# Matmuls on zeros, in thirteen orders of the moving operand, between the warm-up and the first product of a two-block kernel

## The chip, the cores and the metric

One core of a Trainium2 chip runs one program. The metric is the device time of one execution, in microseconds. Before the change it is 2994.82 us, the median of three runs (2993.81 to 2994.98).

## The reference, cut to what matters

256 tokens of 2048 features go through two transformer blocks, in float32:

```python
def forward(x, ...):
    for i in range(2):          # first block: an even layer, then an odd one
        h = rmsnorm(x, g)       # even: sparse top-k and dilated attention; odd: stick-breaking and forgetting
        x = x + (attention(h @ w_in) * silu(gate)) @ w_out
    x = rmsnorm(x, norm_f)
    # second block: swiglu feed-forward, NSA attention beside a gated recurrence, swiglu, per-layer embedding
    ...
```

Nearly all the arithmetic is in the products with the weight matrices. The change adds nothing to what is computed: none of its results is read.

## The kernel before, in words

**Products.** Every weight matrix is cut into panels of up to 512 columns, and a panel into tiles of two chunks of 128 rows (128x1024 values, 512 KB). `run_stream` walks over these tiles in order. The activations are kept transposed, split into a high part `hi` and a rest `lo` (`to_act`, lines 251 to 258: TensorE transposes into PSUM on line 247, ScalarE writes `hi`, VectorE writes `lo`). A weight tile is split in the same way by `cut` (lines 324 and 325: ScalarE writes `wh`, VectorE `wl`). For each chunk and each of the two halves of the tokens, `product` issues three matmuls (lines 366 to 368): hi times wh, hi times wl, lo times wh. So a chunk takes six matmuls, each with 512 float32r columns as the moving operand in contiguous order and its own weight load.

**Order.** The order of the instructions on each engine is the order of the Python code. Work beside the products waits in queues of closures (`soon`, `paced`, `back`) from which `run_stream` takes one at fixed points; after the first chunk of a tile it takes one from `paced`.

**The start.** SyncE's queue first gets the gains `nrow`, then in turn pieces of the input (`load_x`, eight of 256 KB) and the first five weight tiles (`load`, at most `RAWB` = 5 at a time). `start` fills a bfloat16 tile `wu` with zeros on VectorE, and `warm(WARM)` multiplies it with itself eight times (line 525). A transpose then brings the gains into a column layout (`g0T`). After that `run_stream` runs, for i = 0, 1, 2: the transposes and splits of input piece i (`first[i]`), `FILL[i]` = 4, 2, 0 more warm-up matmuls, the load of tile 5 + i and the split of tile i. Then the products begin; the transposes of pieces 3 to 7 come out of `paced`, one per tile.

**Buffers.** Tiles of 128x1024 float32 come out of a pool of 27 (`blk`); PSUM tiles for everything but the products come out of a pool of four (`aux`).

**One other line that the prediction uses.** Line 1345 (`cmp_blocks`) is a VectorE addition far behind the start; it reads every sixteenth value of one tile, and each value of the other operand 15 times. Lines 1223 and 488 are VectorE products over contiguous values.

Of the kernel before, what the change touches and what calls it, by code (L numbers as in the profile page):

```python
# [11 lines left out]
F32 = mybir.dt.float32  # L12
F32R = mybir.dt.float32r
# [6 lines left out]
P = 128  # L20
T = 256
D = 2048
# [13 lines left out]
# columns of the float32 constants  # L36
# [8 lines left out]
# columns of the bfloat16 constants  # L45
# [69 lines left out]
class Act:  # L115
    """Transposed activations, split: chunk c is a pair of [128, 256] float32r views."""
# [8 lines left out]
def two_blocks_kernel(ctx, tc, a, out):  # L125
# [43 lines left out]
    # residual stream, natural: h[p] is [128 tokens, 2, 512 columns]  # L169
# [8 lines left out]
    def load_x(i):  # L178
        """columns of two chunks of x"""
        v = slice(i % 2 * T, i % 2 * T + T)  # L180
        nc.sync.dma_start(h[i // 2][:, :, v], xs[:, :, i * T:i * T + T])
# [20 lines left out]
    def sums(parts, n, s):  # L202
        """room for partial sums of squares [128, 2, parts] and, behind them, n * eps"""
        t = cp.tile([P, 2, parts + 1], F32, name=s)
        nc.gpsimd.memset(t[:, :, parts:parts + 1], n * EPS)
        return t

    def rsq(ssq, s):
        """(sum of the parts of ssq) ** -0.5, as [128, 2]"""
        tot = small([P, 2], s)  # L210
        nc.vector.tensor_reduce(tot, ssq, axis=AX.X, op=ALU.add)
        r = cp.tile([P, 2], F32, name=nm(s))
        nc.gpsimd.tensor_tensor(r, tot, mhalf, op=ALU.pow)
        return r
# [22 lines left out]
    def to_act(src, act, c0, n, gain):  # L237
        """src: natural [128, 2, n * 128]; chunks c0.. of act (within a group of four), scaled per feature by
        gain(c)."""
        hi, lo = act_block(act, c0 // 4)  # L240
        b = c0 % 4
        for j in range(0, n, 2):
            w = min(2, n - j)
            tp = aux()
            for i in range(w):
                for t in range(2):
                    nc.tensor.transpose(tp[:, i * 256 + t * P:i * 256 + t * P + P],  # L247
                                        src[:, t, (j + i) * P:(j + i + 1) * P], ident)
            if gain is None:
                tv = tp[:, :w * 256].rearrange("p (c q) -> p c q", q=256)  # L250
                nc.scalar.activation(hi[:, b + j:b + j + w], tv, AF.Copy)  # L251
                nc.vector.tensor_tensor(lo[:, b + j:b + j + w], tv, hi[:, b + j:b + j + w], op=ALU.subtract)  # L252
            else:
                for i in range(w):
                    nc.scalar.activation(hi[:, b + j + i], tp[:, i * 256:i * 256 + 256], AF.Copy,  # L255
                                         scale=gain(c0 + j + i))
                for i in range(w):
                    nc.vector.scalar_tensor_tensor(lo[:, b + j + i], tp[:, i * 256:i * 256 + 256], gain(c0 + j + i),  # L258
                                                   hi[:, b + j + i], op0=ALU.mult, op1=ALU.subtract)
            for i in range(w):  # L260
                act.hi[c0 + j + i] = hi[:, b + j + i]
                act.lo[c0 + j + i] = lo[:, b + j + i]
# [10 lines left out]
    def panel(w, n0, n1, groups, act, done, coff=0, rate=1, pre=None, late=False, hold=0):  # L273
        # hold: chunks in whose shadow nothing of the paced queue is started
        """x-stationary product of act with w[:, n0:n1]; groups: lists of chunks, in order."""
        panels.append(dict(w=w.rearrange("(c p) n -> p c n", p=P), n0=n0, n1=n1, groups=groups, act=act,
                           done=done, coff=coff, rate=rate, pre=pre, late=late, hold=hold, raw=None))
# [8 lines left out]
    def run_stream():  # L286
# [56 lines left out]
        for s, (pl, cs, first, slot_end, last) in enumerate(tiles):  # L343
# [9 lines left out]
            else:  # L353
# [16 lines left out]
                if n <= P:  # L370
                    # narrow panel, held whole: one tile of tokens after the other
                    held.append((cs, wh, wl))
                    if last:
                        seq = [(c, wh, wl, j) for cs, wh, wl in held for j, c in enumerate(cs)]
                        held = []
                        for t in range(2):
                            for i, x in enumerate(seq):
                                product(t, *x, i == 0, i == len(seq) - 1)
                    cs_ = ()
                else:  # L380
                    cs_ = cs
# [25 lines left out]
    def pipeline(units, depth, between={}):  # L407
        """units: lists of `depth` closures; one closure per slot, each unit's steps in successive slots."""
        for i in range(len(units) + depth - 1):
            def go(i=i):  # L410
                for d in range(depth - 1, -1, -1):
                    if 0 <= i - d < len(units):
                        units[i - d][d]()
            back.append(go)
            if i in between:
                back.append(between[i])

# [1 line left out]
    def softmax_unit(qT, kT, v, bias, evac, mult=None, extra=None, full=False):  # L419
        """qT(), kT(): [128, 256]; v(kt): [128 keys, 128]; bias: [128, 384] bf16 (queries of tile 0 x keys of  # L420
        tile 0 | queries of tile 1 x all keys); evac(t, psum, 1 / sum)."""
# [53 lines left out]
    def rope_nat(src, dst, c0, nh, half, cn, sn, dup=False):  # L475
        """Rotate heads of 2 * half columns at src[:, t, c0:]; write to dst at the same columns."""
# [14 lines left out]
    def heads_T(src, cols, dst, scale=1.0):  # L491
        """Transpose the 128-column slices src[:, t, c] (c in cols) into dst(i): [128, 256]; pairs share a bank."""
# [14 lines left out]
    # =====================================================================  # L507
    # start: gains, input, statistics
    # =====================================================================
# [4 lines left out]

    def start():
        # the clocks of the tensor engine and the activation tables are up before the first data arrive
# [6 lines left out]
        def warm(n):  # L523
            for _ in range(n):
                mm(tpw, wu[:, 0:P], wu, start=True, stop=True)
        warm(WARM)
        tp0 = aux()
# [29 lines left out]
    # =====================================================================  # L557
    # layer_even
    # =====================================================================
# [174 lines left out]
    # residual update by a panel of a product, then the next layer's operand  # L734
# [22 lines left out]
    # =====================================================================  # L757
    # layer_odd
    # =====================================================================
# [94 lines left out]
    def odd_gate(j, c0, c1):  # L854
        """columns c0:c1 of the gate; panel 0 also carries the forget logits in front."""
# [61 lines left out]
    def load_gain(name):  # L917
        """a gain on all partitions, two blocks of 1024 columns"""
# [36 lines left out]
    # =====================================================================  # L955
    # feed-forward layers
    # =====================================================================
# [50 lines left out]
    def post_norm_panel(y, ssq, i, gname, f):  # L1008
        """sums of squares of a finished panel; the panel times the gain and f * sqrt(D)."""
# [12 lines left out]
    def post_norm(y, ssq, last_gain, act, gain, ss_next, rkey):  # L1022
        """h += normed y; next operand, two chunks at a time."""
# [56 lines left out]
    # =====================================================================  # L1080
    # mixer
    # =====================================================================
# [43 lines left out]
    def pre_mix4():  # L1126
        # 8 * softplus(-lambda), with log1p(e) = 2 atanh(e / (2 + e))
# [39 lines left out]
    def rope_part(n, c0, nh):  # L1167
        """rotate the first 32 columns of heads at n[:, t, c0:], in place"""
# [138 lines left out]
    KV = {"kc0": 0, "kc1": 1, "vc0": 2, "vc1": 3, "ks0": 4, "ks1": 5, "kw0": 6, "kw1": 7}  # L1307

    def mix_kv(items, post=None):
        """items: (column, kind, name); k kinds are rotated and transposed, vT transposed, v kept."""  # L1310
# [39 lines left out]
    def cmp_panel(wname, which):  # L1350
        st = {}

        def fn(i, rawt):
# [6 lines left out]
            if i == 7:  # L1360
                # gelu(2y) = (1 + tanh(2 sqrt(2 / pi) (1 + 4 * 0.044715 y^2) y)) y
# [9 lines left out]
                def fin1():  # L1371
# [6 lines left out]
                    def fin2():  # L1378
                        po = aux()
                        w2 = KM["w2"]  # L1380
                        if which == 0:
                            for c in range(2):
                                mm(po[:, 0:30], w2[:, 0, c], hT[:, c], start=c == 0, stop=c == 1)
                            # the keys of head h at columns 16 h .. 16 h + 14 of row block h
# [40 lines left out]
    def nsa_cmp():  # L1425
        """attention to the compressed keys, all heads, added to the other two"""
# [51 lines left out]
    def nsa_heads(j):  # L1478
        """attention of four heads to the selected blocks and to the window"""
# [84 lines left out]
    # =====================================================================  # L1564
    # second feed-forward, per-layer embedding
    # =====================================================================
# [72 lines left out]
```

## Time and profile before

| what | value |
|---|---|
| median of three runs | 2994.82 us (2993.81 to 2994.98) |
| span of the profiled execution, first to last instruction | 2991.7 us |
| time outside the span, by difference to the median | 3.1 us |
| TensorE busy (matmuls) | 2969.3 us, 99% |
| VectorE busy | 1611.1 us, 54% |
| ScalarE busy | 1439.6 us, 48% |
| mean DMA rate | 178 GB/s |

The profile gives no time of its own for the profiled execution beyond the span; the runs are not the profiled execution, and the 3.1 us is a difference between the two. Matmuls are pipelined: the duration of one in the rows reaches past the start of the next one, so the cost of a matmul in a stream is the step from one start to the next, not its duration. In a row that merges several, the time is that from the first start to the last end.

### The profile page before, as it was taken

The page shows a single profiled execution, that of the slowest core. Times are in us where ns is not written, and L with a number is a line of the kernel's source. Part 1 is how long each engine was busy: PE and PEld are TensorE (multiplying, and loading weights), DVE is VectorE, ACT ScalarE, POOL GpSimd, SP SyncE. Part 2 cuts the span into 40 slices and gives each one's busy share as a digit, 9 for nine tenths or more (in the row PEclk, how much of TensorE's full clock was granted, in tenths as well). Part 3 has the DMA queues.
Part 4 walks back from the last instruction along what each step waited for, and adds up shares of the span by engine and source line. Part 5 has one row for each costly group of instructions (what it writes and reads, how often), then busy time and mean ns, then how long its engine had stood idle before and what let it go on. Part 6 is the DMA issues. An engine that isn't in the chain of part 4 may idle for free. (4 is left out here: it accounts for less than half of the span.)

```text
span 2991.7 us, 36158 instructions
## 1 busy us (share of the span) xinstructions
PE 2969.3 (99%) x13805; PEld 2436.2 (81%) x13805; DVE 1611.1 (54%) x2126; ACT 1439.6 (48%) x1961; POOL 38.3 (1%) x83
## 2 busy tenths in 40 slices
PE   9999999999999999999999999999999999999998
PEld 7788888888998888888888887887888888888787
DVE  5675554444455554454454565666644445454565
ACT  5545545484554544443434464555544443443464
POOL 1000000000000000000000010000000000000000
PEclk9999999999999999999999999999999999999999
DMA  7555566646555666656666556644565665656654
GB/s 229 157 173 151 156 183 177 184 140 180 147 180 181 191 182 187 188 183 186 185 185 200 180 156 196 197 152 134 170 183 187 185 189 184 185 185 200 182 171 146
DMA packets 289038, 531.59 MB, mean 178 GB/s; under 512 B 17328, under 2 KB 60704, under 8 KB 288864
## 3 DMA queue, kind: packets, MB, share of 16 engines
q1 hardware_dynamic: 285184, 520.04, 57.8%
q0 software_dynamic: 2960, 8.13, 0.8%
q8 instruction: 108, 1.77, 0.2%
q10 hardware_dynamic: 720, 1.11, 0.1%
q14 instruction: 66, 0.54, 0.1%
HBM read 527.11 MB, written 2.10 MB: 177 GB/s over the span
## 5 line engine op out<-in xcount | busy, mean ns | idle before, releaser
L325 DVE TENSOR_TENSOR wl<-raw,wh 128x1024 fp32r<-128x1024 f32 (+5 forms) x994 | 1184.2, 1198 | 1052.4 <-ACT wh L324 1045.8
L324 ACT ACTIVATE wh<-raw 128x1024 fp32r<-128x1024 f32 (+5 forms) x994 | 1025.1, 1037 | 1097.3 <-PE mm L368 1054.0
L366 PE MATMUL mm<-wh,hi 128*128 128x512 f32 (+4 forms) x3968 | 1548.4, 390 | 1.1 <-ACT hi L255 0.6
L368 PE MATMUL mm<-wh,lo 128*128 128x512 f32 (+4 forms) x3968 | 1547.2, 390 | 1.0 <-DVE lo L258 1.0
L367 PE MATMUL mm<-wl,hi 128*128 128x512 f32 (+4 forms) x3968 | 1535.3, 387 | 1.4 <-DVE wl L325 1.1
L367 PEld LDWEIGHTS mm<-wl,hi 128*128 128x128 f32 x3968 | 746.3, 188 | 165.0 <-DVE wl L325 3.8
L366 PEld LDWEIGHTS mm<-wh,hi 128*128 128x128 f32 x3968 | 746.0, 188 | 157.1 <-issue 3.3
L368 PEld LDWEIGHTS mm<-wh,lo 128*128 128x128 f32 x3968 | 745.6, 188 | 156.5 <-DVE lo L258 2.9
L252 DVE TENSOR_TENSOR lo<-ax,hi 128x512 fp32r<-128x512 f32 x61 | 39.3, 686 | 47.1 <-ACT hi L251 47.1
L251 ACT ACTIVATE hi<-ax 128x512 fp32r<-128x512 f32 x61 | 33.2, 595 | 63.9 <-PE ax L247 63.9
L255 ACT ACTIVATE hi<-ax,gT 128x256 fp32r<-128x256 f32 x72 | 29.5, 472 | 40.4 <-PE ax L247 40.4
L446 ACT ACTIVATE e<-ax,m 128x128 f32<-128x128 f32 x68 | 28.0, 416 | 42.7 <-DVE m L443 42.6
L461 ACT ACTIVATE pT<-ax 128x384 f32<-128x384 f32 x40 | 19.5, 488 | 47.5 <-PE ax L459 47.2
L996 DVE TENSOR_TENSOR y<-mm,y 128x512 f32<-128x512 f32 (+2 forms) x52 | 32.0, 644 | 15.7 <-PE mm L368 15.6
L443 DVE TENSOR_REDUCE m<-ax 128x1 f32<-128x128 f32 x80 | 24.7, 351 | 25.2 <-PE ax L434 17.1
L258 DVE SCALAR_TENSOR_TENSOR lo<-ax,gT,hi 128x256 fp32r<-128x256 f32 x72 | 30.9, 477 | 12.9 <-ACT hi L255 12.8
L229 ACT ACTIVATE junk<-h 128x512 f32<-128x512 f32 x56 | 35.5, 634 | 2.5 <-DVE h L934 1.1
L247 PE MATMUL ax<-cf,h 128*128 128x128 f32 x192 | 29.1, 278 | 7.5 <-DMA h<-in_x_dram 3.6
L247 PEld LDWEIGHTS ax<-cf,h 128*128 128x128 f32 x192 | 23.2, 142 | 15.6 <-issue 6.1
L452 DVE RECIPROCAL rl<-l 128x2 f32<-128x2 f32 x40 | 6.6, 166 | 46.6 <-ACT e L446 46.4
L1359 PE MATMUL ax<-raw,cb 128*30 128x256 f32 x128 | 28.6, 380 | 0.0
L366 PE MATMUL mm<-wh,rhi 128*128 128x512 f32 x64 | 27.6, 431 | 0.0
(392 smaller groups left out, 1231.1 us busy)
## 6 DMA issues: line engine op xcount, KB each, us to landing
raw<-in_w_in_dram SPq DMA_DIRECT2D x239, 512.0 KB, 3.7
raw<-in_ff_w_gate_dram SPq DMA_DIRECT2D x176, 512.0 KB, 3.8
raw<-in_ff_w_up_dram SPq DMA_DIRECT2D x176, 512.0 KB, 3.8
raw<-in_ff_w_down_dram SPq DMA_DIRECT2D x170, 512.0 KB, 3.6
raw<-in_w_out_dram SPq DMA_DIRECT2D x93, 512.0 KB, 4.0
raw<-in_w_ple_gate_dram SPq DMA_DIRECT2D x26, 512.0 KB, 4.3
raw<-in_w_in_dram SPq DMA_DIRECT2D x32, 384.0 KB, 3.6
raw<-in_w_in_dram SPq DMA_DIRECT2D x24, 412.0 KB, 3.5
```

Of the source, the lines that this page charges most:

```text
L229: nc.scalar.activation(j[:, :src.shape[2]], src[:, t], AF.Square, accum_out=ssq[:, t, p:p + 1])
L247: nc.tensor.transpose(tp[:, i * 256 + t * P:i * 256 + t * P + P], src[:, t, (j + i) * P:(j + i + 1) * P], ident)
L251: nc.scalar.activation(hi[:, b + j:b + j + w], tv, AF.Copy)
L252: nc.vector.tensor_tensor(lo[:, b + j:b + j + w], tv, hi[:, b + j:b + j + w], op=ALU.subtract)
L255: nc.scalar.activation(hi[:, b + j + i], tp[:, i * 256:i * 256 + 256], AF.Copy, scale=gain(c0 + j + i))
L258: nc.vector.scalar_tensor_tensor(lo[:, b + j + i], tp[:, i * 256:i * 256 + 256], gain(c0 + j + i), hi[:, b + j + i], op0=ALU.mult, op1=ALU ...
L324: nc.scalar.activation(wh[:, k], v[:, k], AF.Copy)
L325: nc.vector.tensor_tensor(wl[:, k], v[:, k], wh[:, k], op=ALU.subtract)
L366: mm(o, xh[:, q], wh[:, j], start=first, stop=False)
L367: mm(o, xh[:, q], wl[:, j], start=False, stop=False)
L368: mm(o, xl[:, q], wh[:, j], start=False, stop=last)
L996: nc.vector.tensor_tensor(v[:, t], pt[t], v[:, t], op=ALU.add)
```

## The change

Between `warm(WARM)` and the transpose of the gains, `start` calls a new function. It takes two of the 27 blocks (`x` as stationary, `y` as moving operand, float32r), a bfloat16 tile of its own and one PSUM tile, fills the three SBUF tiles with zeros on VectorE, and runs the same list twice: thirteen groups of float32r matmuls, nine in the first group and six in each of the others, then six bfloat16 matmuls. By the code these are 2 x (9 + 12 x 6 + 6) = 174 matmuls. The rest of the diff takes out comments and docstrings.

```diff
+    def strides(out):
+        x, y = blk("px", F32R), blk("py", F32R)
+        xb = cp.tile([P, 512], BF16, name="pxb")
+        nc.vector.memset(x.bitcast(F32), 0.0)
+        nc.vector.memset(y.bitcast(F32), 0.0)
+        nc.vector.memset(xb, 0.0)
+        out2 = aux()
+
+        def run(m, cols=P, n=6, two=False, same=False):
+            size = 1
+            for k in m.shape[1:]:
+                size *= k
+            for i in range(n):
+                o = (out2 if two and i % 2 else out)[0:cols, 0:size]
+                j = 0 if same else i % 4
+                mm(o, x[:, j * P:j * P + cols], m, start=True, stop=True)
+
+        for _ in range(2):
+            run(y[:, 0:512], n=9)
+            run(y[:, 2:514])
+            run(y.rearrange("p (a b) -> p a b", b=32)[:, :, 0:16])
+            run(y.rearrange("p (a b) -> p a b", b=4)[:, :, 0:2])
+            run(y.rearrange("p (a b) -> p a b", b=8)[:, :, 0:4])
+            run(y[:, None, 0:16].to_broadcast([P, 32, 16]))
+            run(y.rearrange("p (s a b) -> p a s b", s=4, b=16)[:, 0:8])
+            run(y.rearrange("p (s a b) -> p a s b", s=2, b=16)[:, 0:16])
+            run(y.rearrange("p (s a b) -> p a s b", s=2, b=2)[:, 0:128])
+            run(y[:, 0:256])
+            run(y[:, 0:512], cols=96)
+            run(y[:, 0:512], two=True)
+            run(y[:, 0:512], same=True)
+            for _ in range(6):
+                mm(out, xb[:, 0:P], xb, start=True, stop=True)
+
     def start():
...
         warm(WARM)
+        strides(tpw)
         tp0 = aux()
         nc.tensor.transpose(tp0[:, 0:16], nrow, ident[0:16, 0:16])
```

Twelve of the thirteen groups have 512 columns, one has 256. Seven read `y` in pieces: runs of 16 values with gaps of 16, runs of 2 with gaps of 2, runs of 4 with gaps of 4, the same 16 values 32 times, runs of 16 from four quarters in turn, runs of 16 from two halves in turn, runs of 2 from two halves in turn.

## Rows read from the trace of the kernel before

**Rows 1.** The page's first part: span; engine, busy us, share, instructions.

```profile
span 2991.7 us, 36158 instructions
PE 2969.3 (99%) x13805; PEld 2436.2 (81%) x13805; DVE 1611.1 (54%) x2126; ACT 1439.6 (48%) x1961; POOL 38.3 (1%) x83
```

**Rows 2.** Busy time by stretch, all engines; the columns are named in the first line.

```profile
core 0: us, PE busy (x) PEld busy (x) DVE busy (x) ACT busy (x) POOL busy (x), PEclk, DMA share, GB/s
5.00:10.00 5.00, 3.15 (x16) 1.78 (x16) 3.19 (x8) 3.71 (x7) 3.04 (x7) 1.00 1.00 337
10.00:15.00 5.00, 2.00 (x10) 1.38 (x10) 3.18 (x4) 1.90 (x3) 2.92 (x19) 1.00 1.04 395
15.00:20.00 5.00, 4.63 (x16) 3.75 (x17) 2.21 (x4) 2.84 (x4) 0.00 (x0) 0.66 1.08 359
500.00:1000.00 500.00, 500.00 (x2423) 425.20 (x2422) 243.14 (x295) 274.66 (x386) 5.92 (x9) 1.00 0.57 170
```

**Rows 3.** Timeline of TensorE's start: start us, us, instruction, [idle before <-releaser].

```profile
1.19 3.60 PE L525 MATMUL ax<-wu 128*128 128x512 bf16 x8 [1.19 <-DVE wu L518]
4.93 1.12 PE L247 MATMUL ax<-cf,h 128*128 128x128 f32 x4
7.70 0.59 PE L525 MATMUL ax<-wu 128*128 128x512 bf16 x2
10.35 0.48 PE L366 MATMUL mm<-wh,hi 128*128 128x512 f32 x1
15.37 0.63 PE L247 MATMUL ax<-cf,h 128*128 128x128 f32 x4 [3.37 <-DMA h<-in_x_dram]
17.08 0.63 PE L367 MATMUL mm<-wl,hi 128*128 128x512 f32 x1
17.50 0.63 PE L368 MATMUL mm<-wh,lo 128*128 128x512 f32 x1
20.18 0.60 PE L247 MATMUL ax<-cf,h 128*128 128x128 f32 x4
20.53 0.48 PE L366 MATMUL mm<-wh,hi 128*128 128x512 f32 x1
```

**Rows 4.** The same view at 500 us: first and last of nine 512-column matmuls.

```profile
499.74 0.39 PE L366 MATMUL mm<-wh,hi 128*128 128x512 f32 x1
501.60 0.40 PE L368 MATMUL mm<-wh,lo 128*128 128x512 f32 x1
```

**Rows 5.** The same view at 1850 us: first and last of nine 384-column matmuls.

```profile
1849.97 0.34 PE L366 MATMUL mm<-wh,hi 128*128 128x384 f32 x1
1851.38 0.34 PE L368 MATMUL mm<-wh,lo 128*128 128x384 f32 x1
```

**Rows 6.** The same view for VectorE and ScalarE in the start.

```profile
0.86 0.27 DVE L518 MEMSET wu<- 128x256 uint32 x1 [0.86 <-PEq L1627]
6.09 0.84 ACT L255 ACTIVATE hi<-ax,g0T 128x256 fp32r<-128x256 f32 x2 [3.41 <-PE ax L247]
7.75 1.28 DVE L325 TENSOR_TENSOR wl<-raw,wh 128x512 fp32r<-128x512 f32 x2
9.85 1.23 DVE L325 TENSOR_TENSOR wl<-raw,wh 128x1024 fp32r<-128x1024 f32 x1
20.82 0.84 ACT L255 ACTIVATE hi<-ax,g0T 128x256 fp32r<-128x256 f32 x2 [1.04 <-PE ax L247]
```

**Rows 7.** What TensorE waited for from 20 us on, the longest: total, times, longest.

```profile
PE ax L247 <- DVE h L1029: 2.0, 2, 1.0
```

**Rows 8.** VectorE by line and shape: busy us, mean ns, idle before.

```profile
L1345 DVE TENSOR_TENSOR cb<-kvT,vT 128x240 f32<-128x240 f32 x8 | 4.1, 559 | 0.2 <-ACT kvT L499 0.2
L1223 DVE TENSOR_TENSOR ig<-ig,xc 128x256 f32<-128x256 f32 x8 | 3.4, 424 | 15.5 <-ACT ig L1222 15.5
L488 DVE TENSOR_TENSOR ne<-ne,cf 128x512 f32<-128x512 f32 x8 | 5.5, 692 | 0.3
```

## The prediction

> **What bounds the kernel now.** I read the page's head first: TensorE's matmuls cover 99% of the span of 2991.7 us, the next engine has 54% [rows 1]. A share is an average, so the stretches come next: between 500 and 1000 us TensorE is busy for all 500.00 us with the DMA queues at 0.57 [rows 2]. What TensorE waits for after the start is small, the longest item 2.0 us in all [rows 7]. So nearly anything put on TensorE's queue lengthens the run by its own time. The exception is the stretch the change goes into. From 5 to 15 us TensorE is busy for 3.15 and 2.00 of each 5 us, with the DMA share at 1.00 and above [rows 2], and the timeline says for what it waits: the piece of the input that lands before 15.37 [rows 3]. From 15 to 20 us the granted clock reads 0.66 on the mean, and matmuls of 512 columns step by 0.42 us (17.08 to 17.50); that is the 1.2 GHz level. Work placed ahead of the first product therefore first eats waiting time, then costs in full.
>
> **The change part by part.**
>
> *The end of the warm-up.* Eight bfloat16 matmuls start at 1.19 and take 3.60 us with the tail of the last [rows 3]. 512 columns at the 1.2 GHz level are 0.427 us, so the ninth could start at 1.19 + 8 x 0.427 = 4.6 us. The added matmuls start there. Their zeros are ready: a fill of 256 words took 0.27 us [rows 6], so two of 1024 words and one of 256 take about 2.4 us behind the 1.13 us at which `wu` is done, that is until 3.6. This leaves 1.0 us of cover; without it the delay would be the excess alone. VectorE has nothing else to do until the gains come.
>
> *The price of one matmul.* In a full stream nine matmuls of 512 float32r columns start from 499.74 to 501.60: 1.86 / 8 = 0.233 us each [rows 4]. With 384 columns eight steps take 1.41, so 0.176 [rows 5]; on that line 256 columns are 0.176 - (0.233 - 0.176) = 0.12. The bfloat16 warm-ups stepped by 0.427 at the 1.2 GHz level, so they take half, 0.21, at the other; two of them in 0.59 with the last one's tail agree [rows 3]. Each added matmul has its own weight load, as these have.
>
> *The orders.* No row shows TensorE reading a moving operand in pieces. The low end is the contiguous price. The high end comes from the nearest row of a reader that gets single values: VectorE's line 1345 reads every sixteenth value, and 240 of them take 559 ns, where 256 contiguous ones take 424 and 512 take 692 [rows 8]. Contiguous values are (692 - 424) / 256 = 1.05 ns each, on a fixed part of 155 ns; the single ones are (559 - 155) / 240 = 1.68 ns. If TensorE paid 1.68 ns for every run that it fetches, the two orders in runs of 2 would need 256 x 1.68 = 0.43 us per matmul in place of 0.233; runs of 4 need 0.215 and longer ones less, so they stay hidden. I take the contiguous price for all orders: another engine's fetch is a far row, and runs of two are not single values. The Trainium skill bears on this (SBUF — State Buffer, section "Door 1: The DMA port swizzle", the box on cachelines): two hits in each 16-byte line are said to be enough for full bandwidth, and every order here takes at least two float32 values of a line. By it the total stays at the forecast; no run here shows it for TensorE.
>
> *Clock.* At 4.93 us four transposes still take 1.12, against 0.60 at 20.18 [rows 3]; so the clock came up after about 5.5 to 6 us. With no pause between the warm-up and the added work I let the first 3 matmuls go at 0.427, from 4.6 to 5.9 us.
>
> *Sum on TensorE.* Of 2 x 87 = 174 matmuls, 150 have 512 float32r columns, 12 have 256 and 12 are bfloat16. 3 x 0.427 + 147 x 0.233 + 12 x 0.12 + 12 x 0.21 = 1.3 + 34.3 + 1.4 + 2.5 = 39.5 us, so the block ends at 4.6 + 39.5 = 44.1 us. If only 163 of them come to run, it is 11 x 0.233 = 2.6 less. The Trainium skill (TensorE: Matmul & The Clock Gate, section "Back-to-back issue gap") has a step of N / 2.4 + 2.5 ns, which is 0.216 for 512 columns. Its sum would be 147 x 0.017 = 2.5 us lower; the trace has 0.233 in every full stretch that I read, and the row decides.
>
> *Restart behind it.* By 44 us every transfer that the start waited for has landed long before (the last wait for input ended at 15.37, and the DMA share had fallen by 500 us to 0.57), so only the chain of engines is left. Transposes take 0.64 to ScalarE's `hi` (20.18 to 20.82) [rows 3, 6]; with the gains' transpose ahead, 0.75. From `hi` at 6.09 to the end of the first half of `wl`, 7.75 + 0.64 = 8.39, are 2.3 us [rows 6]. The products so start 3.05 us behind the block; the remaining warm-ups and transposes (6 x 0.21 + 12 x 0.09) fit into that. Then come six matmuls (1.4), four transposes (0.35, 20.18 to 20.53 [rows 3]), and twelve matmuls (2.8): 7.6 us behind the block, at 51.7, TensorE stands where it stood at 20.18 before. The second tile's `wl` is ready at 9.85 + 1.23 - 6.09 = 5.0 behind `hi`, so 5.75 behind the block, and is wanted at 6.2: a cover of 0.45 us. If a split came late in the restart, it would add up to 2 us.
>
> *What moves with it.* The loads of SyncE wait, as before, for the split of an earlier tile, so the sixth and later ones go out some 30 us later, and TensorE wants them as much later. The two blocks and one PSUM tile shift which buffer each later tile reuses; as the waits behind the start are as small as [rows 7], I put this at 0, with 2 us to either side.
>
> *Total.* 51.7 - 20.2 = 31.5 us more. From there the program is the same, at a full TensorE: span 2991.7 + 31.5 = 3023.2 us, and with the 3.1 us between span and median 2994.8 + 31.5 = **3026.3 us**.
>
> **The rivals.**
>
> A. *Runs of two cost TensorE a fetch each.* 24 matmuls at 0.43 for 0.233: + 4.7, so 3031. For it: line 1345 [rows 8]. Against it: each fetch would still bring two values.
>
> B. *Every broken order goes at half speed.* Seven groups, 84 matmuls, at 0.43: + 16.5, so 3043. For it: nothing in the trace has such an operand, and several orders have three or four levels. Against it: only the single values of line 1345 show any loss, and it is 1.6 times, not 2.
>
> C. *The clock stays at 1.2 GHz, or falls back, during the block.* 150 x 0.427 + 12 x 0.21 + 12 x 0.427 = 71.7 for 39.5: + 32, so 3058. Against it: matmuls on zeros brought the clock up before [rows 3].
>
> D. *Not slower: the matmuls cost next to nothing*, because nothing reads their result and they are dropped or cut short. The place is the wait before 15.37. The delay is the block's time less the 20.2 - 7.6 - 4.6 = 8.0 us that TensorE has to spare there, so it decides at 8.0 us, or 0.046 us a matmul; below that the time is 2995. Against it: the 8, 4 and 2 warm-ups of line 525, which nothing reads either, all run, at 0.427 and 0.21.
>
> **How the numbers follow.** The forecast has 0.62; its own range is 3022 to 3030 (2.6 less if fewer run, 0.45 to 2 more for a late split, 2 either way for buffers). A has 0.17, B 0.11, C 0.04, D 0.02, other causes 0.04. The range 3021 to 3046 takes in the forecast, A and B and leaves C and D out. About 0.2%, or 6 us, is what a measurement of this kernel can tell from no change; only D and part of the other causes lie within it or below: faster 0.01, within 0.02, slower 0.97.
>
> **What would show it.** In the changed kernel's timeline the block starts near 4.6 us, steps by 0.233 in twelve of the thirteen groups and by 0.12 in the one of 256 columns, and ends near 44 us; the first product starts 3 us behind it without a wait for input; the granted clock stays at 1.00 where it read 0.66; and every stage behind has the length that it has now, shifted by 31.5 us. A step of 0.43 in the two orders by runs of 2 shows A, in all seven B, everywhere C. The prediction is wrong if the step depends on the order in a way that neither row suggests, or if the shift behind the start is not constant.

## The result, and the profile after

The changed kernel takes 3029.3 us (median of four, 3028.78 to 3030.16) against 2994.3 for the kernel before on the same chip: 1.0118 times as long, 95% interval 1.0106 to 1.013, or 35.0 us more. The forecast was 3026.3 with its own range to 3030 and a stated range of 3021 to 3046. The direction and nearly all of the size were right. 3.5 us were missing, and most of the miss sits in one step: the price of two of the thirteen orders. The 3029.3 lies inside the forecast's own range, but that range was built for late splits and shifted buffers and not for the price of an order, so its holding is luck.

The head of the page after, to be held against [rows 1] (lines behind 514 have moved by 35 in the changed kernel, those behind the call of the new function by 36):

```profile
span 3026.9 us, 36509 instructions
PE 3009.9 (99%) x13977; PEld 2466.2 (81%) x13979; DVE 1613.3 (53%) x2129; ACT 1439.5 (48%) x1961; POOL 38.4 (1%) x83
```

The stretches that [rows 2] shows of before. TensorE is now busy from 5 to 20 us without a gap, the granted clock reads 1.00 where it read 0.66, and the stage at 500 us has the same 500.00 us and the same 2423 matmuls, 35 us later:

```profile
core 0: us, PE busy (x) PEld busy (x) DVE busy (x) ACT busy (x) POOL busy (x), PEclk, DMA share, GB/s
5.00:10.00 5.00, 5.00 (x21) 4.00 (x20) 0.00 (x0) 0.00 (x0) 2.98 (x6) 1.00 0.99 339
...
15.00:20.00 5.00, 5.00 (x21) 3.70 (x20) 0.00 (x0) 0.00 (x0) 0.00 (x0) 1.00 0.97 321
...
535.00:1035.00 500.00, 500.00 (x2423) 425.19 (x2422) 243.53 (x296) 274.68 (x386) 5.94 (x9) 1.00 0.55 169
```

The timeline of TensorE, which answers to [rows 3]. The third row is six of the matmuls that read runs of 2 with gaps of 2, the fourth six in runs of 4, the fifth six in runs of 2 from two halves:

```profile
4.22 21.34 PE L531 MATMUL ax<-py,px 128*128 128x512 f32 x81
...
8.73 1.61 PE L531 MATMUL ax<-py,px 128*128 128x512 f32 x6
...
10.18 2.90 PE L531 MATMUL ax<-py,px 128*128 128x512 f32 x6
...
12.90 1.57 PE L531 MATMUL ax<-py,px 128*128 128x512 f32 x6
...
18.60 2.13 PE L531 MATMUL ax<-py,px 128*128 128x512 f32 x6
...
48.25 0.23 PE L564 MATMUL ax<-cf,nrow 16*128 16x16 f32 x1
...
56.01 0.60 PE L247 MATMUL ax<-cf,h 128*128 128x128 f32 x4
```

Six matmuls in runs of 16 take 1.61, in runs of 4 1.57; in runs of 2 they take 2.90 and 2.13. That is 1.33 and 0.56 more for each six, 3.8 us over the two passes. The block ends at 48.25, where the gains' transpose starts (forecast 44.1), and the transposes that stood at 20.18 [rows 3] stand at 56.01, 7.76 behind the end of the block (forecast 7.6).

From there the shift is constant up to 1810 us. One line's eight matmuls far behind, before:

```profile
L1471 PE MATMUL ax<-vbd,cpT x8: 592/592/592, 2038.2 to 2068.0; 128*128 128x512 f32 x8
```

and after (the columns are the shortest, median and longest duration in ns, and the first and last start):

```profile
L1507 PE MATMUL ax<-vbd,cpT x8: 592/592/592, 2073.4 to 2103.2; 128*128 128x512 f32 x8
```

The shift is 35.83 at 20.18 us and 35.2 at 2040. Compared start by start over the 994 splits on VectorE it is 35.85 us from 33 to 1810 us, and 35.2 from 1866 to the end; the 0.65 between arises in a stage where the shift changes by another amount in every run (from -0.74 to +0.46 in the seven kernels below).

### The profile page after: what moved, and what is told of

Same layout as the page of the kernel before. It is cut to its first block, busy times and chain, and to the rows that moved or that the text cites. A ratio compares the mean times of both kernels' runs of the same rounds, so it can differ in the third digit from the quotient of the medians.

```text
span 3026.9 us, 36509 instructions
## 1 busy us (share of the span) xinstructions
PE 3009.9 (99%) x13977; PEld 2466.2 (81%) x13979; DVE 1613.3 (53%) x2129; ACT 1439.5 (48%) x1961; POOL 38.4 (1%) x83
## 5 line engine op out<-in xcount | busy, mean ns | idle before, releaser
L531 PE MATMUL ax<-py,px 128*128 128x512 f32 (+2 forms) x162 | 41.8, 421 | 0.0
L531 PEld LDWEIGHTS ax<-py,px 128*128 128x128 f32 (+1 forms) x162 | 30.4, 192 | 11.1 <-issue 3.2
```

The source lines that it names most:

```text
L531: mm(o, x[:, j * P:j * P + cols], m, start=True, stop=True)
```

## The experiments

**e1: the two groups in runs of 2 read contiguously.**

```diff
-            run(y.rearrange("p (a b) -> p a b", b=4)[:, :, 0:2])
+            run(y[:, 0:512])
...
-            run(y.rearrange("p (s a b) -> p a s b", s=2, b=2)[:, 0:128])
+            run(y[:, 0:512])
```

> The changed kernel with its two groups in runs of 2 (24 matmuls) read contiguously instead; all else as changed. Theory (the excess over the forecast lies in these two groups: they step by 0.452 and 0.328 us in the changed kernel's trace, contiguous ones by 0.233): 12 x 0.219 + 12 x 0.095 = 3.8 us less than the changed kernel, so 3025.5 us and a span near 3023. Rival (the excess is the clock at the start, switching between orders and types, or the buffers): no change, 3029.3.

Measured: 3025.4 us (3024.0 to 3025.8) beside 2993.7 for the kernel before, span 3023.1. The end of the block:

```profile
4.23 19.14 PE L531 MATMUL ax<-py,px 128*128 128x512 f32 x81
...
44.17 0.23 PE L564 MATMUL ax<-cf,nrow 16*128 16x16 f32 x1
```

The block ends at 44.17, 4.08 us sooner than in the changed kernel, and the time is 31.6 us above before, where the forecast had 31.5. By the steps in the two traces 3.8 of the 4.08 us are the two groups' (0.452 and 0.327 against 0.232). The other 0.3 is the clock: the second added matmul already steps by 0.35 here, while in the changed kernel the second and third step by 0.43 and the fourth by 0.30, on the same code. So the rival falls as the cause of the excess, and the clock keeps 0.3 us of the difference between these two executions.

**e2: a block of other orders, each group from its own line.** The warm-ups are left out, so that the first groups run at the 1.2 GHz level.

```diff
-            run(y[:, 0:512], n=9)
...
+        for i in range(6):
+            mm(*go(i, ab(4)[:, :, 0:2]), **k)      # line 542; ab(b): y as "p (a b) -> p a b"
+        for i in range(6):
+            mm(*go(i, ab(2)[:, :, 0:1]), **k)      # line 546, and so on
```

> Another block in the place of the added one: no warm-ups, then 22 groups on zeros, each from its own line, six matmuls each (three and nine in two contiguous ones). Theory LINE: each 16-byte line that the moving read goes on to costs 1.77 ns (0.452 us / 256), hidden while that is less than the columns take. Theory RUN: each run (each jump of the address) costs 1.77 ns, whatever line it lies in. Steps in us, LINE / RUN: float32r singles with step 2, 0.45 / 0.91; runs of 4 that straddle two lines 0.45 / 0.23; runs of 6 (85) 0.30 / 0.23; the same pair 256 times 0.23 / 0.45; 256 singles one to a line 0.45 / 0.45; 128 pairs 0.23 / 0.23; bfloat16 pairs with gaps of 2 (two to a line) 0.23 / 0.45, with gaps of 6 0.45 / 0.45; bfloat16 singles with step 2 0.23 / 0.91, with step 4 0.45 / 0.91. Pairs from two halves in turn 0.33 again (neither theory gives that), from four quarters open. Pairs at the 1.2 GHz level, at the start: 0.45 if the cost is a fixed time, 0.9 if it goes with TensorE's clock.

The timeline of TensorE. A step is the distance between the starts of two following rows, by the count; where the type of the operand changes, the first record behind starts too early for this (in the changed kernel the block's first is at 4.22, 0.07 us behind the start of the last warm-up), and a step is taken between the single matmuls of one row. Of lines that read alike one or two are shown:

```profile
3.34 1.65 PE L534 MATMUL ax<-py,px 128*128 128x512 f32 x3 [3.34 <-DVE px L519]
4.78 2.90 PE L536 MATMUL ax<-py,px 128*128 128x512 f32 x6
7.51 1.57 PE L538 MATMUL ax<-py,px 128*128 128x512 f32 x6
8.92 2.21 PE L540 MATMUL ax<-py,px 128*128 128x512 f32 x9
10.97 2.88 PE L542 MATMUL ax<-py,px 128*128 128x512 f32 x6
...
16.39 2.90 PE L546 MATMUL ax<-py,px 128*128 128x512 f32 x6
19.11 2.90 PE L548 MATMUL ax<-py,px 128*128 128x512 f32 x6
21.82 1.99 PE L550 MATMUL ax<-py,px 128*128 128x510 f32 x6
...
26.34 1.49 PE L554 MATMUL ax<-py,px 128*128 128x512 f32 x6
27.67 1.56 PE L556 MATMUL ax<-py,px 128*128 128x256 f32 x6
29.05 1.58 PE L558 MATMUL ax<-py,px 128*128 128x256 f32 x6
30.45 2.18 PE L560 MATMUL ax<-py,px 128*128 128x512 f32 x6
32.46 2.85 PE L562 MATMUL ax<-py,px 128*128 128x512 f32 x6
...
37.97 1.52 PE L568 MATMUL ax<-pb 128*128 128x512 bf16 x6
39.33 2.87 PE L570 MATMUL ax<-pb 128*128 128x512 bf16 x6
```

| line | order | 16-byte lines | step, us |
|---|---|---|---|
| 540 | contiguous | 128 | 0.23 |
| 542, 544 | pairs, gaps of 2, the first two or the middle two values of the line | 256 | 0.45 |
| 546 | singles, step 2 | 256 | 0.45 |
| 548 | runs of 4 across two lines | 256 | 0.45 |
| 550 | 85 runs of 6 | 170 | 0.30 |
| 552 | 255 pairs, each across two lines | 256 | 0.45 |
| 554 | one pair, 256 times | 1 | 0.22 |
| 556 | 256 singles, step 4 | 256 | 0.23 |
| 558 | 128 pairs, one to 32 bytes | 128 | 0.23 |
| 560 | pairs, two halves in turn | 128, each twice | 0.33 |
| 562 | pairs, four quarters in turn | 128, each twice | 0.45 |
| 564 | runs of 4, two halves in turn | 128 | 0.25 |
| 568, 572 | bfloat16, four columns of each line | 128 | 0.23 |
| 570, 574 | bfloat16, two columns of each line | 256 | 0.45 |

LINE holds where the two theories part: singles with step 2 cost 0.45 and not 0.91, runs of 4 that straddle cost 0.45 and not 0.23, and the bfloat16 orders that take four columns from a line in two or four jumps cost nothing. RUN falls. Two rows speak against LINE as well: 256 singles, one to a line, took 0.23 and not 0.45, and pairs from two halves in turn 0.33, where 128 lines would be hidden.

The first rows also show the clock's part: contiguous matmuls at the 1.2 GHz level step by 0.43 (line 534, as the warm-ups in [rows 3]; the granted clock reads 1.00 in that stretch all the same, so only the steps tell the level at the start), and the pairs behind them by (7.51 - 4.78) / 6 = 0.455. By line 538 the clock is up (0.23); where in the six pairs it rose, their steps of 0.45 to 0.46 do not show. The first follows a contiguous matmul of 0.43, and in e6, which starts alike, contiguous matmuls keep the 0.43 until 8.4 us. None of the six took the 0.9 that a multiple of the column time would give, so the cost of the pairs is a fixed time; at the lower clock it is nearly hidden.

**e4: the list once instead of twice.**

```diff
-        for _ in range(2):
+        for _ in range(1):
```

> The added list once instead of twice. Theory (the block first eats the wait for input, 12.4 us of its end, then costs in full): the second pass took 21.5 us, so the block ends at 26.7 and the time is 21.5 us below that of the changed kernel, 3007.8, 13.5 above that of before. Rival (cost in proportion, nothing hidden): half of 35.0, 3011.8.

Measured: 3007.7 us (3006.8 to 3008.0) beside 2993.7, 1.0045 times the kernel before (1.0033 to 1.0058). In proportion it would have been 3011.2 beside that. The block ends 0.6 us later than expected:

```profile
27.30 0.23 PE L564 MATMUL ax<-cf,nrow 16*128 16x16 f32 x1
```

The transposes of 20.18 stand at 35.07, again 7.77 behind it. So the part that a block pays is what goes beyond the wait for input, as the forecast had it, and the second pass, 20.95 us in the traces, is paid in full (35.0 - 14.0 = 21.0).

**e5: a block shorter than the wait.**

```diff
-        for _ in range(2):
-            run(y[:, 0:512], n=9)
...
+        run(y[:, 0:512], n=22)
```

> A block of 22 contiguous matmuls instead of the list. Theory: it ends at 10.5 us, the products can start at 13.6 and wait for the input that lands at 15.3, and with no long pause the clock stays up, so TensorE is at 18.4 where it was at 20.18 before: 1.8 us less than before, 2992.5, at any rate within 0.1% of before. Rival (each matmul costs in full): 4 x 0.427 + 18 x 0.233 = 5.9 us more than before, 3000.2.

Measured: 2992.1 us (2991.2 to 2993.1) beside 2993.7, ratio 0.9995 (0.9986 to 1.0004): 22 matmuls cost nothing that can be told. The trace has more:

```profile
4.23 6.15 PE L531 MATMUL ax<-py,px 128*128 128x512 f32 x22
...
16.07 0.63 PE L247 MATMUL ax<-cf,h 128*128 128x128 f32 x4 [1.07 <-DMA h<-in_x_dram]
...
19.33 0.60 PE L247 MATMUL ax<-cf,h 128*128 128x128 f32 x4
```

The transposes stand at 19.33 instead of 20.18: 0.85 us won, where 1.8 were expected. The clock stayed up as expected (16.07 to 19.33 is 3.26 for what took 4.81 from 15.37 on [rows 3]), but the piece of the input landed for 16.07 instead of 15.37.

**e6 and e8: what the step depends on.** The same frame as e2 with other groups; e6 without the warm-ups, e8 with them and six contiguous matmuls behind each group.

```diff
+        for i in range(6):
+            mm(*go(i, y[:, None, 0:12].rearrange("p u (s q) -> p u s q", q=4)[:, :, :, 0:2].to_broadcast([P, 85, 3, 2])), **k)
...
+            mm(*go(i, ab(4)[:, None, :, 0].to_broadcast([P, 2, 256])), **k)
```

> A third block of groups on zeros in the place of the added one. It settles what the step depends on where the second block left it open (256 singles, one to a line, took 0.233, where 1.77 ns for each line gives 0.45). Theory COLUMN: a column costs 0.45 ns where four columns in a row come out of one 16-byte line, otherwise 0.88 ns, however few come out of a line; a line that is still held counts as the same line. Theory LINE: 1.77 ns for each new line. Steps in us, COLUMN / LINE: 512 float32r singles one to a line (step 4, 8 or 32), 0.45 / 0.91; bfloat16 singles one to a line the same; bfloat16 runs of 3, one to a line, 170 of them, 0.45 / 0.30; bfloat16 runs of 4, one to a line, 0.23 / 0.23; bfloat16 runs of 6, one to a line, 85 of them, 0.30 / 0.23. Pairs out of the same 2, 3, 4 or 8 lines in turn: 0.23 for as many lines as the reader holds, 0.45 beyond; pairs from three thirds in turn between the 0.33 of two and the 0.44 of four. Weight loads with the stationary operand one and two to a line: open, the step of 128 columns is 0.11 where it is contiguous, 0.22 if the same rule holds there.

Lines 536, 538 and 540 are float32r singles with step 4, 8 and 32, line 548 is 85 bfloat16 runs of 6 (one to a line), 550 the pairs from three thirds in turn, 552 to 558 the pairs out of 2, 3, 4 and 8 lines in turn:

```profile
8.45 2.93 PE L536 MATMUL ax<-py,px 128*128 128x512 f32 x6
11.20 2.77 PE L538 MATMUL ax<-py,px 128*128 128x512 f32 x6
...
26.13 1.45 PE L548 MATMUL ax<-pb 128*128 128x510 bf16 x6
27.23 2.60 PE L550 MATMUL ax<-py,px 128*128 128x510 f32 x6
29.65 1.50 PE L552 MATMUL ax<-py,px 128*128 128x512 f32 x6
30.99 1.48 PE L554 MATMUL ax<-py,px 128*128 128x510 f32 x6
32.30 2.84 PE L556 MATMUL ax<-py,px 128*128 128x512 f32 x6
```

LINE, as a plain count of lines, falls with the singles: 512 lines step by 0.46 and 0.43, not 0.91. COLUMN falls with line 548: the runs of 6 take less than 0.22 a step, not 0.30; 85 lines are hidden. Two and three lines in turn cost nothing (0.22), four and eight cost the full 0.45: in these rows the reader acts as if it held three lines. The bfloat16 groups of 3 and of 1 in this block ran across a fall of the clock (0.69 granted from 16.4 to 21.8 us, 0.50 from there to 24.3), so e8 repeats them.

> The eight warm-ups, then groups of six matmuls on zeros, each followed by six contiguous ones that show the clock. Open from the block before: whether float32r singles one to a line cost half of what bfloat16 ones do. Theory PAIRED (float32r columns are fetched two at a time, a fetch of up to two new lines costs 1.77 ns; bfloat16 pays 1.77 ns for each line): 512 float32r singles with step 4 or 8, 0.45; bfloat16 runs of 3 (170 lines) 0.30; bfloat16 singles one to a line 0.90. Rival (the clock had fallen in those groups): float32r singles 0.90 or anything else, bfloat16 runs of 3 0.45. Plain float32 (not r), 512 columns: contiguous 0.43 as in line 1471 of the kernel before; pairs with gaps of 2 and singles open: 0.45 if the second pass hides the fetch, 0.9 if each pass pays it.

Lines 537 and 541 are 512 float32r singles with step 4 and 8, 545 bfloat16 runs of 3, 549 bfloat16 singles one to a line, 553, 557 and 561 plain float32 contiguous, in pairs and in singles (two records to a matmul); 551 are six contiguous float32r:

```profile
7.36 2.93 PE L537 MATMUL ax<-py,px 128*128 128x512 f32 x6
...
11.50 2.75 PE L541 MATMUL ax<-py,px 128*128 128x512 f32 x6
...
15.47 1.97 PE L545 MATMUL ax<-pb 128*128 128x510 bf16 x6
...
18.66 5.56 PE L549 MATMUL ax<-pb 128*128 128x512 bf16 x6
23.18 3.55 PE L551 MATMUL ax<-py,px 128*128 128x512 f32 x6
26.57 5.32 PE L553 MATMUL ax<-py,px 128*128 128x512 f32 x12
...
33.12 5.57 PE L557 MATMUL ax<-py,px 128*128 128x512 f32 x12
...
39.89 10.96 PE L561 MATMUL ax<-py,px 128*128 128x512 f32 x12
```

Float32r singles step by 0.46 and 0.43. In lines 545 to 561 the type changes from row to row, and the steps are those within a row: bfloat16 runs of 3 by 0.30, bfloat16 singles by 0.90 (six in 5.56 us, the last one's 1.08 included). PAIRED holds, and the clock is not the reason: the contiguous matmuls behind the float32r singles and the runs of 3 step by 0.23. PAIRED also gives the 0.23 of e2's 256 singles, which are 128 pairs of columns. A plain float32 pass takes 0.43 contiguous, 0.45 in pairs and 0.90 in singles: each pass pays for its lines, and pairs are hidden behind its slower columns.

**e7: the clock kept up without a block.** The kernel before, with one change:

```diff
+            elif i == LOOK:
+                def kept(go=go):
+                    warm(15)
+                    go()
+                paced.append(kept)
```

> The kernel before (without the added block), with 15 more bfloat16 warm-ups on zeros queued where TensorE waits for the input after its first six product matmuls (11.8 to 15.4 us), ahead of the fourth piece's transposes. Theory (the rest of what the short block won is the clock, which then stays up): the stretch from 15.4 to 20.2 takes 3.2 us instead of 4.8, so 1.6 us less in the trace from 20 us on, 2992.1; in the times within what can be told from no change. Rival (the input sets the pace there, not the clock): no change in the trace either.

Measured: 2993.1 us beside 2993.6, ratio 0.9998 (0.9989 to 1.0007), and in the trace no gain either: the transposes stand at 20.54.

```profile
10.55 0.63 PE L247 MATMUL ax<-cf,h 128*128 128x128 f32 x4 [2.41 <-DMA h<-in_x_dram]
...
12.74 0.63 PE L368 MATMUL mm<-wh,lo 128*128 128x512 f32 x1
13.17 4.28 PE L525 MATMUL ax<-wu 128*128 128x512 bf16 x15
17.29 0.60 PE L247 MATMUL ax<-cf,h 128*128 128x128 f32 x4
...
20.54 0.60 PE L247 MATMUL ax<-cf,h 128*128 128x128 f32 x4
```

The stretch behind it did shrink to 3.25 us as the theory said, but the price was missed: the clock fell soon behind the earlier wait of 2.41 us (products step by 0.23 at 11.26 and by 0.43 from 11.89), so the first few of the 15 warm-ups went at the lower level, and they ran until 17.29, past the 15.37 at which the input was there before. So the rival, that the input sets the pace, is not excluded by this run. Neither this nor e5 beats the kernel before by what its times can tell.

## Why the prediction was right, and where it was not

- *TensorE bounds the run, and the start has room.* Right. The shift is constant to 0.02 us from 33 to 1810 us, and e4 and e5 put the room where the forecast had it: one pass costs 14.0 us, not 17.5, and 22 matmuls cost nothing that the times can tell. Rival D, matmuls that cost next to nothing, is excluded by the 35.0 us.
- *The end of the warm-up, the count and the contiguous price.* Right. The first added matmul is recorded at 4.22 and steps by 0.79, 0.36 us of which is the last warm-up's; so the block takes TensorE over at 4.58, for a forecast of 4.6. e1's block ends at 44.17 for a forecast of 44.1, but by two misses that cancel: the clock came up 0.3 us sooner there than taken, and the four orders in runs of 16 stepped by 0.24 and not 0.233, 0.35 us in all. All groups ran (the 163 of the prediction have no source on record), and only single records of bfloat16 matmuls are missing from the trace.
- *The orders: "I take the contiguous price for all orders".* This is the step that failed. The two groups in runs of 2 cost 3.8 us more than contiguous ones (e1), for 0 taken. It is rival A, which stood at 4.7 us: the far row, VectorE's 1.68 ns for a single value [rows 8], was nearly the price of a line on TensorE, 1.77 ns (0.452 us / 256). No run shows that the two engines pay for the same thing, and the 1.68 rests on line 488 as contiguous, one operand of which repeats its values; that it came so near may be luck. What A had wrong is the unit: it is not the run but the line that counts, so runs of 4 would have cost 0.45 had they not been aligned (e2, line 548). Pairs from two halves, in which each line comes twice, cost 0.33 and not 0.43; by lines alone they would have been free, and why they are not stays open. Rival B is excluded: five of the seven broken orders step by 0.23 to 0.24.
- The Trainium skill (SBUF — State Buffer, section "Door 1: The DMA port swizzle") asks for at least two hits in a line for full bandwidth, and adds that each access that crosses to a new line pays a penalty; I read the first half as "two are enough" and let it weigh against A. At the 2.4 GHz level two are not enough here: pairs, with two hits in each line, step by 0.45 and contiguous columns by 0.23; four columns of a line are needed, in float32r as in bfloat16 (lines 568 to 574 of e2). The measurement decides.
- *Clock.* Right to 0.1 us: three matmuls went at the 1.2 GHz level and a fourth in part (0.30). Rival C is excluded by the steps of 0.23; the granted clock of 1.00, which the prediction named as a sign, does not tell by itself, since it reads 1.00 from 0 to 5 us too, where the warm-ups step by 0.427.
- *Restart.* Right: 7.76 for 7.6, with no split late and no wait for input.
- *Buffers.* Right at 0. The 0.65 us that came back near 1850 us is part of what the runs differ by there.

So 31.5 + 3.8 (runs of 2) + 0.3 (runs of 16) + 0.1 (clock) + 0.15 (restart) = 35.85, the shift of the trace up to 1810 us; less 0.65 (the stage at 1850) it is 35.2, and 35.0 was measured between the medians.

## What to carry to other kernels

On TensorE at the 2.4 GHz level a moving operand cost columns or lines, whichever took longer: count the 16-byte lines that its access pattern goes on to, times 1.77 ns, against 0.45 ns a column. Runs that fill whole lines (4 or 16 aligned float32r columns) were free, 85 runs of 6 took 0.30 us, pairs with gaps doubled the time. The count fails in two places: float32r singles, one to a line, cost half of it, and pairs from distant places in turn cost more. Where no row shows an operation, keep a row from another engine in the range, and ask which unit it is paid for; here the nearest row came within 0.1 ns of the price, which one case cannot show to be more than luck. And work put ahead of a wait for input is paid only for what outlasts the wait; here the wait took up about 8 us.

## What the runs showed of the hardware

- Float32r singles, one to a line, cost 0.84 to 0.90 ns each and bfloat16 ones 1.76 (e8, lines 537, 541 and 549). That float32r columns are fetched two at a time was the theory that foretold it; no run shows the fetch itself.
- Pairs from two, three and four distant places in turn step by 0.33, 0.38 and 0.44 (e2, lines 560 and 562; e6, line 550), though two and three neighbouring lines in turn cost nothing; why two and three places lie between hidden and full stays open.
- The clock fell while TensorE was busy without a gap. In e8 the stretch that ends the bfloat16 singles of 0.90 and holds what follows has 0.79, and the six contiguous matmuls of line 551 step by 0.43, at the 1.2 GHz level; e6 shows the same behind its bfloat16 singles. The float32 singles of the same step (line 561) did not bring it down. Why, no run shows.

```profile
22.00:30.00 8.00, 8.00 (x17) 3.91 (x16) 0.00 (x0) 0.00 (x0) 0.00 (x0) 0.79 0.01 2
...
40.00:52.00 12.00, 12.00 (x19) 3.34 (x17) 0.00 (x0) 0.00 (x0) 0.00 (x0) 1.00 0.00 0
```

- A stationary operand read with step 4 (e6, line 562) has weight loads of 326 ns, where those of line 564, with step 2, take 199; matmuls of 128 columns then step by 0.23 instead of 0.12.

```profile
L562 PEld LDWEIGHTS ax<-py,px 128*128 128x128 f32 x6 | 1.5, 326 | 0.0
...
L564 PEld LDWEIGHTS ax<-py,px 128*128 128x128 f32 x6 | 0.8, 199 | 0.0
```
